# Hybrid state-space and attention layer: branch products per weight block over all tokens, and a later gate for half a branch

## The chip, the cores and the metric

The kernel runs on one core of a Trainium2 chip. The metric is the device time of one launch in microseconds, as the median of several runs. Each engine of the core (PE for matmuls, DVE for vector work, ACT for scalar functions and copies, POOL for the rest, SP for issuing transfers) executes its own instructions in the order in which the program was compiled, and engines wait for each other through semaphores. Matmul results land in PSUM, in banks of 512 float32 columns; all other tiles are in SBUF.

## The reference, cut to what matters

One step of a layer over two streams: 1024 new tokens of one sequence and 64 tokens of a running one, laid side by side as T = 1088 columns.

```python
xn = _rmsnorm(x, p['norm_mix_w'])
z, xbc, dt_raw, q, k, v, gate_ssm, gate_att = split(xn @ p['w_in'])
...
def step(state, inp):
    acum = jnp.cumsum(dtc * a_neg, axis=1)
    seg = acum[:, :, None] - acum[:, None, :]
    decay = jnp.exp(jnp.where(causal, seg, -jnp.inf))
    xdt = xc * dtc[..., None]
    cb = jnp.einsum('blgn,bsgn->blsg', cc, bc)
    y = jnp.einsum('blsg,blsge,bsgep->blgep', cb, decay, xdt)
    y = y + jnp.einsum('blgn,bgepn->blgep', cc, state) * jnp.exp(acum)[..., None]
    to_end = jnp.exp(acum[:, -1:] - acum)
    state = state * jnp.exp(acum[:, -1]) + jnp.einsum('blgn,blge,blgep->bgepn', bc, to_end, xdt)
...
y_ssm = _rmsnorm((y_ssm + d * xs) * silu(z), p['ssm_norm_w'])      # per group of 512
o = _rmsnorm(_diff_attention(q, k_all, v_all, ...), p['subln_w'])  # per head of 128
mix = sigmoid(gate_ssm) * (y_ssm @ p['w_branch_ssm']) + sigmoid(gate_att) * (o @ p['w_branch_attn'])
x = x + mix @ p['w_out']
x = x + conv_ffn(_rmsnorm(x, p['norm_ffn_w']))
```

All inputs and outputs are float32.

## The kernel before, in words

Everything is held feature-major: features on the 128 partitions, tokens along the free axis. Float32 precision is reached by splitting both operands of a product into a rounded part (`hi`) and the rest (`lo`): `product` (L140) issues three matmuls per block of 128 features, hi x hi, hi x lo, lo x hi. A product with 1024 features has 24 matmuls into one PSUM bank. `weights` (L125) loads one 128x1024 weight block (512 KB), casts it on ACT (L136) and subtracts on DVE (L137), into two rotating buffers, with a raised scheduling priority. `acc` (L112) hands out PSUM banks; after the first stage it has two (`pm`).

The stages follow one another roughly so: norm of x, values and time steps, q and k heads, attention (about 560 to 1160 us in the trace), the state-space scan (about 1120 to 1580 us), the branch products, the output product with the second norm (1691 to 1800), the feed-forward part (to the end). The program is a list in priority order; a scheduler with a simulated timeline fixes the order of each engine's instructions when the kernel is built. Work without close dependences is handed out by generators as filler: `fill` (L470) takes a number of steps from the current `filler` after each step of the attention or the scan. In the scan the filler is first what is left of the input projection (`stream`) and, from the tenth of 12 spans on (`BRANCH_AT` = 9), `branch_tiles` (L756); the scheduler may start its work earlier when PE would be idle.

**The scan.** `scan` (L731) goes through 4 groups of 8 heads and 3 spans of 384, 384 and 320 tokens. Each span has 3 calls of `step` (L658), one per 128 tokens (the last has 64), and ends with `gated` (L714). A step loads `bc`, the cumulated decay exponents of 8 heads broadcast over the partitions (L663, 512 KB), and `e2`, their exponentials, two broadcasts to 64 partitions each from the scratch `e_sc` (L664 to L668). PE transposes the inputs (L671, L673) and forms the token products (L674). DVE scales the transposed inputs by the time step into `xdt` and by time step and decay into `xw` (L681). POOL masks `bc` (L682), ACT exponentiates it per head (L684), DVE multiplies (L685), PE forms `yi` (L689), `ye` (L696) and the state update (L702). `e2` multiplies `ye` (L697). `gated` norms the span's output over a group: squares, PE sums (L724), `rstd_of` (L726), four multiplications (L728), a store to `y_sc` (L729).

**The root chain.** `rstd_of` (L209) computes 1/sqrt(mean + eps): ACT Ln (L212) and Exp (L213) for a first value r, then four DVE operations (L214 to L217) for one Newton correction. It is used in the first norm, in the q and k heads (L333), in `gated` and in the second norm (L816).

**The branches.** `branch` (L156) runs three times: attention output `o_sc` with `wba` (branch 1), the first half of the state-space output `y_sc[:D]` with `wbs[0]` (branch 2), both as filler in the scan, and the second half `y_sc[D:]` with `wbs[1]` (branch 3, L784), after the scan. The tokens are cut into two halves of 544. For each half the input is brought into SBUF as 8 blocks of rows, hi and lo (`bring`, L160): branch 1 reads both from `o_sc`; branches 2 and 3 load a staged tile `b_f` (three buffers of 272 columns), cast it on ACT (L169) and subtract on DVE (L170). The tiles `b_hi` and `b_lo` have two buffers, so a later half can come in while an earlier one is multiplied: the second half's rows are issued behind the gate load of weight blocks 2 to 7 (L187 to L190). For each half and each of 8 weight blocks, the gate tile is loaded into `b_g` (L183), for branches 2 and 3 also the running sum (L185), the weight block is loaded and split (L186), and two products of 272 columns follow. DVE reads each result from PSUM as (gate + 1) * product (L196), adds the running sum (L198), and `out` stores it: branch 1 to `m_sc`, branch 2 to `n_sc`, branch 3 through `mixed` (L779), which splits it into hi and lo for the output product. (The stored gate is tanh(g/2); gate + 1 is twice the sigmoid, and the output product is halved at L805.)

Of the kernel before, what the change touches and what calls it, by code (L numbers as in the profile page):

```python
# [42 lines left out]
BG = 4  # L43
LAG = 2
QR = 10
QSQ = 1
BF = 3
# [29 lines left out]
def hybrid_layer(ctx: ExitStack, tc: tile.TileContext, xT, prm, cst, rope, wvd, win, wbs, wba, wout, wup, wdn,  # L77
# [18 lines left out]
    a_sc, e_sc = scratch("a_sc", [32, T]), scratch("e_sc", [32, T])  # L96
# [59 lines left out]
    def branch(stage, pair, src, wts, g0, add, out):  # L156
        def octet():
            return [br.tile([P, 8, HALF], R32, name=n, tag=n, bufs=2) for n in ("b_hi", "b_lo")]

        def bring(c, k, hi, lo):  # L160
            if stage is None:
                for u, t in enumerate((hi, lo)):
                    load(out=t[:, k].bitcast(F32), in_=src[D * u + P * k : D * u + P * (k + 1), c : c + HALF])
                return
            for a in (0, HALF // 2):
                q = slice(a, a + HALF // 2)
                t = stage()
                load(out=t, in_=src[P * k : P * (k + 1), c + a : c + a + HALF // 2])
                S.copy(hi[:, k, q], t)  # L169
                V.tensor_tensor(out=lo[:, k, q], in0=t, in1=hi[:, k, q], op=ALU.subtract)  # L170

        parts = [octet(), None]
        for k in range(8):
            bring(0, k, *parts[0])
        for x, c in enumerate((0, HALF)):
            hi, lo = parts[x]
            if x == 0:
                parts[1] = octet()
            for m in range(KT):
                r = slice(P * m, P * (m + 1))  # L180
                two = pair()
                gt, at = two[:, :HALF], two[:, HALF:T]
                first = load(out=gt, in_=g_sc[g0 + P * m : g0 + P * (m + 1), c : c + HALF])  # L183
                if add is not None:
                    load(out=at, in_=add[r, c : c + HALF])  # L185
                w_hi, w_lo = weights(wts[m], KT, P)  # L186
                if x == 0 and m >= LAG:  # L187
                    with tc.issue_after(first.ins):
                        for k in range(8 * (m - LAG) // (8 - LAG), 8 * (m - LAG + 1) // (8 - LAG)):
                            bring(HALF, k, *parts[1])  # L190
                for a in (0, HALF // 2):
                    q = slice(a, a + HALF // 2)
                    ps = acc(HALF // 2)
                    product(ps, [(w_hi[:, k], w_lo[:, k], hi[:, k, q], lo[:, k, q]) for k in range(KT)])
                    with tc.high_priority(ahead):
                        V.scalar_tensor_tensor(gt[:, q], gt[:, q], 1.0, ps, ALU.add, ALU.mult)  # L196
                if add is not None:
                    V.tensor_tensor(out=gt, in0=gt, in1=at, op=ALU.add)  # L198
                out(m, c, gt)
                yield  # L200

    def store(dst):
        return lambda m, c, t: load(out=dst[P * m : P * (m + 1), c : c + HALF], in_=t)
# [16 lines left out]
    dt_tok, dtw, nacum, decs = (dq.tile([P, 9, 32], F32, name=n) for n in ("dt_tok", "dtw", "nacum", "decs"))  # L220
# [14 lines left out]
    with tc.tile_pool(name="nx", bufs=1) as nx:  # L235
        S.preload_act_table_set(LN_EXP)
        c = 0
        for x, w in enumerate(NORM):
# [6 lines left out]
            if x == 0:  # L245
                load(out=par, in_=prm)
            for k in range(KT):
# [43 lines left out]
    with tc.tile_pool(name="qk", bufs=1) as qk:  # L291
# [66 lines left out]
        def steps():  # L358
# [29 lines left out]
            af, ef = row("af")[:32], row("ef")[:32]  # L388
            for c, w in WIDE:
# [250 lines left out]
    with tc.tile_pool(name="sp", bufs=1) as sp, tc.tile_pool(name="pss", bufs=1, space=PSUM) as pss:  # L640
# [17 lines left out]
        def step(g, ch, o, bx, xs, y, state):  # L658
# [18 lines left out]
            xdt = sp.tile([P, 8, 64], F32, name="xdt", tag="xdt", bufs=2)  # L677
            xw = sp.tile([P, 8, 64], F32, name="xw", tag="xw", bufs=2)
            tr3 = tr[:L].rearrange("p (e q) -> p e q", e=8)
            for dst, sc in ((xdt, dt_tok), (xw, dtw)):  # L680
                V.tensor_tensor(out=dst[:L], in0=tr3, in1=sc[:L, ch, h8].unsqueeze(2).to_broadcast([L, 8, 64]), op=ALU.mult)  # L681
# [71 lines left out]
        def pair():  # L753
            return bs.tile([P, T], F32, name="b_g", tag="b_g", bufs=BG)
# [237 lines left out]
```

## Time and profile before

| what | value |
|---|---|
| median of 3 runs | 2579.67 us (2579.16 to 2581.6) |
| the profiled execution | 2582.58 us, its span 2580.8 us |
| busy: PE, DVE, ACT, POOL | 2525.0, 1399.8, 1032.2, 290.0 us |
| HBM read, written | 263.56 MB, 100.27 MB |
| granted TensorE clock, mean | 0.995 |
| L136, L137 (weight cast, subtract), 220 each | 229.3 us, 284.9 us |
| matmuls on `b_hi` and `b_lo`, 2304 | 228.0 + 227.2 + 227.5 us |

All times of the page are from one profiled execution; the runs' times are without a profile. A matmul's own duration overlaps with the next one's, so counts times start-to-start distance give PE's need, not counts times duration. Idle time of an engine matters only where another one waits for it. The "idle before" column names the instruction that ended the wait.

### The profile page before, as it was taken

To read this page: it belongs to the slowest core of one execution; us is meant where nothing else is said; L and a number is where in the kernel's file an instruction comes from. 1 tells how busy PE (TensorE), PEld (TensorE's weight loads), DVE (VectorE), ACT (ScalarE), POOL (GpSimd) and SP (SyncE) were. 2 spreads that over 40 slices of the span, in tenths; PEclk is the share of its full clock that TensorE was granted. 3 is DMA by queue.
4 is the path that set the end of the run, shared out by engine and by line. 5 is a ranking of instruction groups with operands and counts; after the bars stand their busy time and mean duration, and the time that the engine had idled before them with its cause. 6 is when DMAs were issued, how large, how long until landed. Compare 5 with 4: busy or idle time off the path is not lost.

```text
span 2580.8 us, 41810 instructions
## 1 busy us (share of the span) xinstructions
PE 2525.0 (98%) x16484; PEld 2444.8 (95%) x16484; DVE 1399.8 (54%) x2371; ACT 1032.2 (40%) x2113; POOL 290.0 (11%) x387
## 2 busy tenths in 40 slices
PE   8999999999999999999999989999999999999999
PEld 7999999999999999988788879999999999999999
DVE  7326266654447674665679997658333333343333
ACT  5334234544445554565456643335312222131221
POOL 3000001000001110022333430023000000000000
PEclk9999999999999999999999999999999999999999
DMA  5217167545435433176798978555311111111112
GB/s 162 83 54 282 51 257 213 153 142 148 131 126 164 136 112 111 64 232 192 245 332 258 304 246 272 195 187 193 119 42 47 44 42 50 42 50 40 44 43 77
DMA packets 233685, 366.59 MB, mean 142 GB/s; under 512 B 31184, under 2 KB 160464, under 8 KB 233360
## 3 DMA queue, kind: packets, MB, share of 16 engines
q1 hardware_dynamic: 233488, 363.91, 44.2%
q8 instruction: 130, 2.13, 0.3%
q14 instruction: 67, 0.55, 0.1%
HBM read 263.56 MB, written 100.27 MB: 141 GB/s over the span
## 4 chain that ended last, share of the span: by engine, by line
PE 43%; DMA 3%; DVE 3%; ACT 1%; issue 1%; SPq 0%; POOL 0%; DVEq 0%; ACTq 0%; POOLq 0%
PE mm L143 7%; PE mm L145 7%; PE mm L144 7%; PE up L143 7%; PE up L145 7%; PE up L144 7%; DMA in<-x_sc 1%; DMA b_hi<-o_sc 1%; DVE w_lo L137 1%; PE yi L689 1%; PE stp L702 0%; ACT bc L684 0%; DVE y L728 0%; DMA in<-z_sc 0%; DVE b_lo L170 0%
## 5 line engine op out<-in xcount | busy, mean ns | idle before, releaser
L143 PE MATMUL mm<-xn_hi,w_hi 128*128 128x320 f32 (+1 forms) x1496 | 497.9, 333 | 2.3 <-ACT zr L428 1.1
L145 PE MATMUL mm<-xn_hi,w_lo 128*128 128x320 f32 (+1 forms) x1496 | 496.8, 332 | 0.0
L144 PE MATMUL mm<-xn_lo,w_hi 128*128 128x320 f32 (+1 forms) x1496 | 494.6, 331 | 0.0
L136 ACT CAST w_hi<-w_f 128x1024 fp32r<-128x1024 f32 (+2 forms) x220 | 229.3, 1042 | 547.2 <-PE mm L144 369.3
L137 DVE TENSOR_TENSOR w_lo<-w_f,w_hi 128x1024 fp32r<-128x1024 f32 (+2 forms) x220 | 284.9, 1295 | 300.8 <-ACT w_hi L136 298.4
L143 PE MATMUL up<-x_hi,w_hi 128*128 128x384 f32 (+1 forms) x1056 | 345.0, 327 | 2.7 <-ACT x_hi L820 2.7
L144 PE MATMUL up<-x_lo,w_hi 128*128 128x384 f32 (+1 forms) x1056 | 344.8, 327 | 0.0
L145 PE MATMUL up<-x_hi,w_lo 128*128 128x384 f32 (+1 forms) x1056 | 343.3, 327 | 0.0
L143 PEld LDWEIGHTS mm<-xn_hi,w_hi 128*128 128x128 f32 x1496 | 281.9, 188 | 7.9 <-issue 2.8
L145 PEld LDWEIGHTS mm<-xn_hi,w_lo 128*128 128x128 f32 x1496 | 281.6, 188 | 2.9 <-issue 1.9
L144 PEld LDWEIGHTS mm<-xn_lo,w_hi 128*128 128x128 f32 x1496 | 281.8, 188 | 2.6 <-issue 1.3
L143 PE MATMUL mm<-b_hi,w_hi 128*128 128x272 f32 x768 | 228.0, 298 | 19.1 <-DVE b_g L196 15.9
L144 PE MATMUL mm<-b_lo,w_hi 128*128 128x272 f32 x768 | 227.2, 296 | 0.7 <-DMA b_lo<-o_sc 0.7
L145 PE MATMUL mm<-b_hi,w_lo 128*128 128x272 f32 x768 | 227.5, 297 | 0.0
L143 PEld LDWEIGHTS up<-x_hi,w_hi 128*128 128x128 f32 x1056 | 198.7, 188 | 3.1 <-ACT x_hi L820 3.0
L144 PEld LDWEIGHTS up<-x_lo,w_hi 128*128 128x128 f32 x1056 | 198.8, 188 | 0.1
L145 PEld LDWEIGHTS up<-x_hi,w_lo 128*128 128x128 f32 x1056 | 198.5, 188 | 0.0
L880 DVE TENSOR_TENSOR xa<-xa,mm 128x384 f32<-128x384 f32 x144 | 76.5, 531 | 197.3 <-PE mm L145 197.3
L144 PE MATMUL mm<-f_lo,w_hi 128*128 128x384 f32 (+1 forms) x528 | 173.1, 328 | 0.0
L143 PE MATMUL mm<-f_hi,w_hi 128*128 128x384 f32 (+1 forms) x528 | 173.0, 328 | 0.0
L145 PE MATMUL mm<-f_hi,w_lo 128*128 128x384 f32 (+1 forms) x528 | 173.0, 328 | 0.0
L143 PEld LDWEIGHTS mm<-b_hi,w_hi 128*128 128x128 f32 x768 | 147.3, 192 | 25.4 <-DVE b_g L196 15.4
(252 smaller groups left out, 4803.7 us busy)
## 6 DMA issues: line engine op xcount, KB each, us to landing
w_f<-in_win_dram SPq DMA_DIRECT2D x76, 512.0 KB, 4.0
w_f<-in_wup_dram SPq DMA_DIRECT2D x44, 512.0 KB, 3.7
bc<-a_sc SPq DMA_DIRECT2D x32, 512.0 KB, 6.3
w_f<-in_wbs_dram SPq DMA_DIRECT2D x32, 512.0 KB, 4.2
b_g<-g_sc SPq DMA_DIRECT2D x48, 272.0 KB, 4.5
w_f<-in_wout_dram SPq DMA_DIRECT2D x24, 512.0 KB, 3.8
x_sc<-cc SPq DMA_DIRECT2D x48, 192.0 KB, 1.9
kh_t<-k_st SPq DMA_DIRECT2D x32, 272.0 KB, 6.9
```

The lines of the kernel that those rows point to most:

```text
L136: S.copy(hi, w)
L137: V.tensor_tensor(out=lo, in0=w, in1=hi, op=ALU.subtract)
L143: PE.matmul(ps, a_hi, b_hi, start=i == 0, stop=False)
L144: PE.matmul(ps, a_hi, b_lo, start=False, stop=False)
L145: PE.matmul(ps, a_lo, b_hi, start=False, stop=i == n - 1)
L689: PE.matmul(yi[u : u + 64, e // 2, :L], xdt[:L, e], bc[:L, e, :L], start=True, stop=True)
L880: V.tensor_tensor(out=xa[:, m, c : c + w], in0=xa[:, m, c : c + w], in1=ps, op=ALU.add)
```

## The change: what it does

- `branch` no longer cuts the tokens into two halves. Its input is brought as three pieces of 384, 384 and 320 tokens, all before the first product in program order, each with one buffer per piece (`b_hi0`, `b_lo0` and so on). The loop over weight blocks is outermost, so each block is loaded and split once per branch and serves all three pieces. `TURNS` puts blocks 0 and 1 together, then 2, 3, 4, 5 alone, then 6 and 7 together; in a pair each piece is used for both blocks before the next piece.
- Every product has 384 or 320 columns. `b_f` and `b_g` become tiles of 384 columns; `b_g` has 8 buffers, one tile per load. The generator yields once per product and piece, 24 times a branch instead of 16.
- Branch 2 has no gate and no running sum: ACT copies the product from PSUM, and it is stored to `n_sc`. Branch 3 adds `n_sc` to its product, multiplies by (gate + 1), and adds `m_sc`.
- `rstd_of` computes the correction with one ACT Square and two DVE operations; its result has the opposite sign, and the columns of the norm weights (both norms of x, the state-space norm, the q and k norms) are negated once, by three DVE operations after the parameters' load.
- `e_sc` is gone. `e2` is computed by ACT from `bc`, two exponentials of 64 partitions and 4 x 128 columns, before POOL masks `bc`.
- `dt_tok` and `dtw` lie in one tile, and one DVE operation writes `xdt` and `xw`.

```diff
-BG = 4
-LAG = 2
+BG = 8
+TURNS = ((0, 1), (2,), (3,), (4,), (5,), (6, 7))
...
+    def branch(stage, side, src, wts, gates, adds, out):
+
+        parts = [[br.tile([P, 8, w], R32, name=f"{n}{x}", tag=f"{n}{x}") for n in ("b_hi", "b_lo")]
+                 for x, (c, w) in enumerate(WIDE)]
+        for (c, w), (hi, lo) in zip(WIDE, parts):
+            for k in range(8):
+                if stage is None:
+                    for u, t in enumerate((hi, lo)):
+                        load(out=t[:, k].bitcast(F32), in_=src[D * u + P * k : D * u + P * (k + 1), c : c + w])
+                else:
+                    t = stage()[:, :w]
+                    load(out=t, in_=src[P * k : P * (k + 1), c : c + w])
+                    S.copy(hi[:, k], t)
+                    V.tensor_tensor(out=lo[:, k], in0=t, in1=hi[:, k], op=ALU.subtract)
+        for ms in TURNS:
+            wt = [weights(wts[m], KT, P) for m in ms]
+            for (c, w), (hi, lo) in zip(WIDE, parts):
+                for m, (w_hi, w_lo) in zip(ms, wt):
+                    beside = []
+                    for d, r0 in ([(g_sc, gates)] if gates is not None else []) + [(d, 0) for d in adds]:
+                        t = side()[:, :w]
+                        load(out=t, in_=d[r0 + P * m : r0 + P * (m + 1), c : c + w])
+                        beside.append(t)
+                    to = beside[0] if beside else side()[:, :w]
+                    ps = acc(w)
+                    product(ps, [(w_hi[:, k], w_lo[:, k], hi[:, k], lo[:, k]) for k in range(KT)])
                     with tc.high_priority(ahead):
-                        V.scalar_tensor_tensor(gt[:, q], gt[:, q], 1.0, ps, ALU.add, ALU.mult)
-                if add is not None:
-                    V.tensor_tensor(out=gt, in0=gt, in1=at, op=ALU.add)
-                out(m, c, gt)
-                yield
+                        if not beside:
+                            S.copy(to, ps)
+                        elif not adds:
+                            V.scalar_tensor_tensor(to, to, 1.0, ps, ALU.add, ALU.mult)
+                        else:
+                            V.tensor_tensor(out=beside[1], in0=beside[1], in1=ps, op=ALU.add)
+                    if adds:
+                        V.scalar_tensor_tensor(to, to, 1.0, beside[1], ALU.add, ALU.mult)
+                        V.tensor_tensor(out=to, in0=to, in1=beside[2], op=ALU.add)
+                    out(m, c, to)
+                    yield
...
         act(u, mean, AF.Ln, bias=eps_t[: out.shape[0]], scale=scale)
         act(r, u, AF.Exp, scale=-0.5)
-        V.tensor_scalar(u, mean, -0.5 * scale, -0.5 * EPS, ALU.mult, ALU.add)
-        V.tensor_tensor(out=u, in0=u, in1=r, op=ALU.mult)
-        V.tensor_tensor(out=u, in0=u, in1=r, op=ALU.mult)
-        V.scalar_tensor_tensor(out, u, 1.5, r, ALU.add, ALU.mult)
+        act(u, r, AF.Square, scale=math.sqrt(0.5 * scale))
+        V.scalar_tensor_tensor(u, mean, EPS / scale, u, ALU.add, ALU.mult)
+        V.scalar_tensor_tensor(out, u, -1.5, r, ALU.add, ALU.mult)
...
                 load(out=par, in_=prm)
+                for a, b in ((O_MIX, O_CW), (O_SN, O_D), (O_QN, O_FW)):
+                    V.tensor_scalar_mul(par[:, a:b], par[:, a:b], -1.0)
...
-                act(ef[:, c : c + w], pf[:32, :w], AF.Exp)
             load(out=a_sc, in_=af)
-            load(out=e_sc, in_=ef)
...
-            ev = e_sc.rearrange("(j u) t -> u j t", u=2)
             for u in range(2):
-                src = ev[u, 4 * g : 4 * g + 4, c0 : c0 + L].unsqueeze(0).to_broadcast([64, 4, L])
-                load(out=e2[64 * u : 64 * u + 64, :, :L], in_=src)
+                half = slice(64 * u, 64 * u + 64)
+                act(e2[half, :, :L], bc.rearrange("p (j u) t -> p u j t", u=2)[half, u, :, :L], AF.Exp)
...
-            for dst, sc in ((xdt, dt_tok), (xw, dtw)):
-                V.tensor_tensor(out=dst[:L], in0=tr3, in1=sc[:L, ch, h8].unsqueeze(2).to_broadcast([L, 8, 64]), op=ALU.mult)
+            V.tensor_tensor(out=xx[:L], in0=tr3, in1=dtt[:L, :, ch, h8].unsqueeze(3).to_broadcast([L, 2, 8, 64]), op=ALU.mult)
...
-            yield from branch(None, pair, o_sc, wba, D, None, store(m_sc))
-            yield from branch(stage, pair, y_sc[:D], wbs[0], 0, m_sc, store(n_sc))
+            yield from branch(None, side, o_sc, wba, D, (), store(m_sc))
+            yield from branch(stage, side, y_sc[:D], wbs[0], None, (), store(n_sc))
...
-    run(branch(stage, pair, y_sc[D:], wbs[1], 0, n_sc, mixed))
+    run(branch(stage, side, y_sc[D:], wbs[1], 0, (n_sc, m_sc), mixed))
```

More of the change, by code (lines that the diff above doesn't have):

```diff
@@ L202, in store @@
     def store(dst):
-        return lambda m, c, t: load(out=dst[P * m : P * (m + 1), c : c + HALF], in_=t)
+        return lambda m, c, t: load(out=dst[P * m : P * (m + 1), c : c + t.shape[1]], in_=t)
     def run(gen):
@@ L387, in steps @@
             V.tensor_tensor(out=dtw, in0=dtw, in1=dt_tok, op=ALU.mult)
[L388 removed]
+            af = row("af")[:32]
             for c, w in WIDE:
@@ L750, in stage, with side @@
         def stage():
-            return bs.tile([P, HALF // 2], F32, name="b_f", tag="b_f", bufs=BF)
-        def pair():
-            return bs.tile([P, T], F32, name="b_g", tag="b_g", bufs=BG)
+            return bs.tile([P, 384], F32, name="b_f", tag="b_f", bufs=BF)
+        def side():
+            return bs.tile([P, 384], F32, name="b_g", tag="b_g", bufs=BG)
         def branch_tiles():
```

51 lines of the change are left out of this document (8 added, 43 removed).

## The prediction

> **What bounds the kernel now.** The page comes first: it says that PE is busy 98% of the span, but a busy share cannot say how fast the matmuls follow one another. So the stage table comes next, cut where the first matmul on a `b_hi` piece starts (1265.7), where branch 3 starts (1594.5) and where it ends (1691).
>
> ```profile
> 1265.70:1594.50 328.80, 304.47 (x2373) 273.70 (x2374) 287.15 (x411) 176.61 (x355) 119.33 (x74) 0.97 0.89 287
> 1594.50:1691.00 96.50, 96.50 (x769) 96.50 (x768) 58.67 (x95) 32.49 (x47) 0.00 (x0) 1.00 0.60 195
> ...
> 1800.00:2581.00 781.00, 777.41 (x4704) 777.14 (x4704) 287.76 (x443) 184.99 (x291) 29.07 (x86) 1.00 0.16 53
> ```
>
> The columns are PE, PEld, DVE, ACT, POOL, granted clock, DMA share, GB/s. Branches 1 and 2 and two thirds of the scan share 328.8 us in which DVE is 87% busy, the DMA engines 89%, and the clock drops below 1. Branch 3 and the feed-forward part run with nothing in PE's way. The timeline of PE gives the true price of a matmul, which is start to start:
>
> ```profile
> 1600.16 0.29 PE L143 MATMUL mm<-b_hi,w_hi 128*128 128x272 f32 x1
> 1600.28 0.28 PE L144 MATMUL mm<-b_lo,w_hi 128*128 128x272 f32 x1
> ...
> 1900.15 0.34 PE L143 MATMUL mm<-f_hi,w_hi 128*128 128x384 f32 x1
> 1900.32 0.34 PE L144 MATMUL mm<-f_lo,w_hi 128*128 128x384 f32 x1
> ...
> 1904.75 0.31 PE L143 MATMUL mm<-f_hi,w_hi 128*128 128x320 f32 x1
> 1904.90 0.31 PE L144 MATMUL mm<-f_lo,w_hi 128*128 128x320 f32 x1
> ```
>
> Over longer runs this is 0.1255 us for 272 columns (320 matmuls in the 40 us from 1640), 0.173 for 384 and 0.146 for 320; the lines' 0.29 to 0.34 are latency. What holds PE up between 1265.7 and 1594.5 is read from its waits, and from the clock around the gaps:
>
> ```profile
> PE mm L143 <- DVE b_g L196: 15.9, 8, 4.6
> PE tr L671 <- ACT in L653: 2.8, 4, 1.2
> PE yi L689 <- DVE bc L685: 1.6, 1, 1.6
> ```
>
> (us in total, times, longest), and
>
> ```profile
> 1384.00:1391.00 7.00, 5.85 (x26) 5.85 (x27) 2.73 (x5) 0.73 (x3) 0.00 (x0) 0.51 0.64 196
> ...
> 1304.00:1309.00 5.00, 4.43 (x23) 4.47 (x24) 4.96 (x8) 4.39 (x10) 2.97 (x2) 0.66 1.09 361
> 1532.00:1538.00 6.00, 5.27 (x26) 4.77 (x26) 6.00 (x11) 0.89 (x1) 0.03 (x1) 0.72 0.96 313
> ```
>
> One wait stands out: PE has two accumulation banks, and eight times it finds both unread because DVE is behind with L196. The clock then falls: 7 x 0.49 + 5 x 0.34 + 6 x 0.28 = 6.8 us lost on top of the 15.9. The timeline puts 8.7 us of the waits (2.5, 4.6, 1.6) and the first two dips (5.1 us) into branch 1, and 7.2 us and 1.7 us into branch 2. What DVE does there:
>
> ```profile
> L137 DVE TENSOR_TENSOR w_lo<-w_f,w_hi 128x1024 fp32r<-128x1024 f32 x31 | 51.8, 1672 | 2.9 <-ACT w_hi L136 2.8
> ...
> L170 DVE TENSOR_TENSOR b_lo<-b_f,b_hi 128x272 fp32r<-128x272 f32 x48 | 28.4, 618 | 3.9 <-ACT b_hi L169 3.9
> ...
> L196 DVE SCALAR_TENSOR_TENSOR b_g<-b_g,mm 128x272 f32<-128x272 f32 x63 | 26.6, 426 | 10.0 <-PE mm L145 9.9
> ```
>
> So branch 1, branch 2 and the scan are bound by PE's amount of work plus some 45 us of stalls: 64 products x 24 x 0.1255 = 193 us, 24.5 scan steps x about 3.6 us and nine L724 pairs of 0.5 us make 92 us (a step from the timeline: tr 0.44, cb 0.33, yi 1.0, ye 0.8, stp 0.86, some 0.2 for the changes between them), so 285 of 328.8.
>
> **The change, part by part.** *Piece widths.* Per weight block 4 x 24 x 0.1255 = 12.05 us become 48 x 0.173 + 24 x 0.146 = 11.81. Over 24 blocks that is **-5.9 us** of PE, about 2 per branch. *Weight blocks used once.* 48 loads with their L136 and L137 become 24. In the stage that takes away 16 x 1.67 = 27 us of DVE, 16 x 1.04 = 17 us of ACT, 8.4 MB. *Branch 2 ungated.* L196 (32 x 0.43) and L198 (16, 13 us) leave DVE, 27 us; ACT takes 24 reads of PSUM at about 0.45 (L428, 128x320: 0.428). Gate and m_sc loads, 32 x 0.28 = 9 MB, leave the stage; branch 3 adds m_sc. *Root chain.* Nine times L214 to L217 (0.53 + 0.62 + 0.63 + 0.76) become two DVE operations of about 0.7 and one ACT of 0.5: -10 us of DVE, +4.5 of ACT. *One scaling for xdt and xw.* 25 x (0.68 + 0.675) becomes one operation of 1024, taken at 1.22 by L543's 128x1024 read of PSUM: -3.4 us. *Branch 3's prefetch* (16 L170, 10 us) leaves the stage, since single buffers forbid it. DVE goes from 287 to about 287 - 27 - 27 - 10 - 3 - 10 = 210 us, 66% of a stage of 318. *Decay from rows.* 25 x 2 loads of e_sc (6 MB) go; ACT gets 50 exponentials of 64 x 512, each between 0.38 (L684, 128 elements) and 1.42 (L720, mostly 1536); taken 0.58 from L700, whose 512 elements are the nearest: +29 us (+71 at the upper end, ACT then at 76%, still beside PE's work). ACT ends near 177 - 17 + 11 + 4.5 + 29 - 6 = 199 us, 62%: hidden. DMA falls by 8.4 + 9 + 6 + 2 of 94 MB.
>
> On the path each step waits longer: bc's landing (6.8 us), then the two exponentials (1.2 us), then POOL's L682, since L682 overwrites bc. ACT is in order, so weight casts and branch 2's evacuations queue behind an exponential whose bc is late. L684 waits 34.8 us for L682 already, with three bc buffers ahead of it and branch matmuls to cover it: **0**, bounds -3 (DVE's wait of 1.1 for e_sc and some landing time go) and +10.
>
> *What DVE's relief gives.* Branch 2's banks are read by ACT: 7.2 + 1.7 us go. In branch 1 DVE still reads them, with a quarter less to do: half of 13.8. **-16 us**, bounds 0 and -22.7. A page of the Trainium skill weighs the dips otherwise: TensorE: Matmul & The Clock Gate, Part 1, halves the clock after an idle window of about 3.4 us. By that alone only the 4.6 us gap would cost its dip, 3.4 of the 6.8 us, and the gain would be 7.2 and half of 12.1, 13 us for 16 (sum -7.4); the trace has dips behind gaps of 2.5 and 2.2 us, and decides.
>
> *Pieces held once.* The three pieces of a branch have one buffer each, so the next branch can fill a piece only after blocks 6 and 7 have used it. Bringing 24 blocks of rows through three b_f buffers costs c / 3 each, with c a buffer's round from issue over landing and L169 to the end of L170. In the quiet of branch 3 c is 5.2 us (third load of a set at 1605.9, its subtract over at 1611.1), in the scan about 10 (1462.8 to 1473.4). Covered are about 50 us (15.3 of products after piece 0 is free, 7 of scan; then two pieces of 8.3 with 8 of scan beside; the first products of piece 2 the rest). Branch 2 stalls by 8c - 50: nothing at 5.2, 30 at 10. DVE and DMA a quarter lighter put c near 7.2: **+8 us**. Branch 3 meets no scan: piece 0 is free 15.3 us ahead, piece 2 is asked for 16.6 us after branch 2's end, 32 us in all, and 24 x 5.2 / 3 = 42 less the last piece's own work and the three loads in flight gives **+3** (bounds 0 and +10). Branch 1 needs 3.1 MB before its first product instead of 4.4, but all 8.7 MB in its first 24 us of products instead of half: **0**, bounds -5 and +8.
>
> *Weight handover.* After the pair (0, 1), and into the next branch, a new block's cast and subtract (1.04 + 1.22 quiet, 1.67 busy) must fit into one 320-wide product of 3.5 us, where 6 us were free before. Waits on L136 are 1.5 us now: **+2**, bounds 0 and +6. *Elsewhere* the last L212 chain before the feed-forward part and the first norm lose one DVE operation each (0.5 and 0.4), both head blocks about as much: **-1.5**. The negated parameter columns wait for par (lands 9.0 us in) in a DVE gap from 8.3 to 10.8: **0**, up to +2 if they are put ahead of the squares. Branch 3's DVE work rises to 24 x (0.55 + 0.6 + 0.55 + 0.55) + 13 + 10 = 77 of 97 us, PSUM reads first: **0**, up to +5.
>
> Sum: -5.9 - 16 + 8 + 3 + 2 - 1.5 = **-10.4**. The profiled execution took 2582.58 us (span 2580.8, 1.8 around it), 2.9 above the median of the runs, 2579.67; the same difference on the median gives **2569.3**.
>
> **Rivals.** *A: everything opens up* (chance 0.23). With DVE at two thirds all waits for L196 and their dips go (-22.7), half of the stage's other PE idle time of about 12 us goes (-6), and rounds of 5 to 6 us stall nothing: with -5.9 and -1.5 that is -36, **2543.5**. For it: branch 3 and the feed-forward part show PE without gaps where DVE is 61% and 37% busy. Against it: from 1160 to 1260 DVE is at 48%, and PE still loses some 10 us in small waits behind scan steps.
>
> *B: slower, at the start of branch 2* (0.22). With c at 10, as in the scan now, the stall is 30 instead of 8: +22, **2591**. It decides from c = 8.5, where 8c - 50 eats the -10.4. For it: DMA landings in the scan have a median of 5.6 us for 136 KB, and the new loads are 192 KB; the subtract that frees a buffer stands behind scan work in DVE's order. Against it: today's rounds belong to prefetches that nobody waits for.
>
> *C: nothing to measure* (0.15): the scan itself, through POOL and ACT (L684 behind L682 34.8 us, now behind two more exponentials), paces branch 2, and DVE's freed time is idle; about half the -16 goes, with +3 of extra stall: **2580**.
>
> **How the numbers follow.** The forecast has 0.40, its own range 2562 to 2577. A measurement tells apart about 0.2%, 5 us. Faster: 0.35 of the forecast and A, 0.58. Within: 0.04 and C's 0.14, 0.18. Slower: B and the ends, 0.24. The range runs from A's centre to B's, 2544 to 2591, and leaves a tenth beyond each.
>
> **What would show it.** PE's wait for the first product's bank in the stage falls from 15.9 us to under 8; branch 3's products start near 1584 instead of 1594.5 and take about 97 us; DVE's share of the stage is near 66%; c is 6 to 8 us. PE waiting for `b_hi` or `b_lo` by over 20 us makes the prediction wrong on B's side, exponentials waiting for bc with PE idle on C's.

## The result, and the profile after

The changed kernel takes 2603.18 us (median of 4 runs, 2601.23 to 2605.43), the kernel before 2580.64 us on the same chips: a ratio of 1.0086 with a 95% interval of 1.0074 to 1.0098. It is slower by 22 us where 10 us less were forecast, and it lies outside the range. One launch each of the kernel before, of e4 and of e5 was far slower (8752, 3065 and 3509 us) and is left out of the numbers below. The profiled executions differ by 20.4 us of span (2601.2 against 2580.8), so the profile can be asked where they went.

A table of the times at which PE reaches the same instruction in both traces answers most of it:

| PE reaches | before | after | later by |
|---|---|---|---|
| the first projection matmul | 20.0 | 26.8 | 6.8 |
| the first `mm<-xn_hi,w_hi` (the q and k heads, behind values and time steps) | 83.3 | 89.1 | 5.8 |
| the 81st score matmul of the attention | 495.3 | 505.9 | 10.6 |
| the scan's first `yi` | 1131.9 | 1145.8 | 13.9 |
| the first product on `b_hi` | 1265.7 | 1272.4 | 6.7 |
| the scan's last `yi` | 1545.9 | 1537.6 | -8.3 |
| the output product | 1691.1 | 1713.7 | 22.6 |
| the end | 2580.8 | 2601.2 | 20.4 |

(The attention begins earlier than the 560 us given above: its first score matmul before the change is at 410.0.) Two stretches lose time: everything up to the scan (13.9 us) and the branch stage itself (441.3 us for 425.4, +15.9). Half of the first loss comes back before the branches begin: from the scan's first `yi` to the first product on `b_hi` PE takes 126.6 us for 133.8. Of the experiments below, e5 and e8, which compute the decay factors from `bc`, take 126.9 and 127.1 us there, e3 and e6, which load them again, 132.5 and 131.8; so this gain goes with the decay rows. The feed-forward part gives 2 us back.

First the stage table of the changed kernel, cut at the first product on `b_hi`, at the start of branch 3 and at its end. The columns are PE, PEld, DVE, ACT, POOL, granted clock, DMA share, GB/s:

```profile
1272.40:1616.60 344.20, 306.64 (x1994) 271.24 (x1994) 224.79 (x287) 210.20 (x412) 113.20 (x74) 0.95 0.64 204
1616.60:1713.70 97.10, 96.02 (x577) 94.86 (x578) 64.10 (x113) 25.67 (x45) 0.00 (x0) 1.00 0.66 205
```

DVE fell from 87% to 65% of the first window, as forecast (66%), and the DMA share from 0.89 to 0.64. Yet PE stands for 37.6 us of it instead of 24.3, and the mean clock is lower (a part of its half-clock time falls into PE's own waiting). Two busy resources were relieved, and the engine that sets the end waits longer. Branch 3 needs 97.1 us, as forecast. The waits of PE in the same stretch (us in total, times, longest) say for whom it stands:

```profile
PE mm L143 <- DVE b_g L186: 15.2, 2, 13.3
PE tr L665 <- ACT in L648: 8.0, 5, 3.6
PE ye L689 <- DVE state L702: 4.6, 3, 2.4
PE cb L667 <- ACT in L648: 3.5, 1, 3.5
```

The wait for DVE's read of PSUM (L186, before L196) is still 15 us, but eight waits have become essentially one, of 13.3 us. It ends at 1316.7. SP's part of the timeline shows what was late (start, duration, instruction; L164 loads a block of rows, L177 a gate tile):

```profile
1304.05 0.58 SPq L164 DMA_DIRECT2D b_hi<-o_sc  x1
1304.67 0.53 SPq L164 DMA_DIRECT2D b_lo<-o_sc  x1
1305.24 0.69 SPq L177 DMA_DIRECT2D b_g<-g_sc  x1
```

All 48 loads of the three pieces stand in SP's queue ahead of the first gate tile: from 1269.95 to 1305.2, 35 us. PE begins the first product at 1272.4, has filled its two banks by 1291.7, does the scan steps that are ready, and stands from 1303.4: no result can be read without a gate. And when the gate has landed (6.2 us after its issue, at 1311.5), DVE is in the span's closing work for another 4.6 us:

```profile
1307.80 8.36 DVE L721 SCALAR_TENSOR_TENSOR y<-y,par,grs 128x384 f32<-128x384 f32 x4
1316.09 0.54 DVE L186 SCALAR_TENSOR_TENSOR b_g<-b_g,mm 128x384 f32<-128x384 f32 x1
...
1307.38 3.67 POOL L712 TENSOR_TENSOR y<-y,in 128x1536 f32<-128x1536 f32 x1 [2.32 <-DVE y L711]
1311.00 1.41 POOL L675 TENSOR_SCALAR_AFFINE_SELECT bc<-bc 128x1024 f32<-128x1024 f32 x1
1312.64 1.84 POOL L714 TENSOR_TENSOR in<-in 128x768 f32<-128x768 f32 x1 [0.23 <-ACT in L713]
1314.56 1.19 POOL L715 TENSOR_TENSOR in<-in 128x384 f32<-128x384 f32 x1
```

Four multiplications that fill 2.20 us when nothing of POOL runs beside them (at 1331.05) fill 8.36 us beside POOL's operations. Each of the four ends 0.41 or 0.42 us after one of the four POOL operations above; the first takes 3.66 us, beside the 3.67 us of L712. The Trainium skill (SBUF — State Buffer, "Who interferes with whom") says that a VectorE instruction with two SBUF inputs contends with a GpSimd instruction that reads SBUF, and calls the ports that they share an exclusive lock; these rows agree, and here it is VectorE that waits.

The other loss is at the very start. SP's queue before, and after:

```profile
11.73 1.38 SPq L242 DMA_DIRECT2D xc<-in_xT_dram  x3
13.15 0.43 SPq L135 DMA_DIRECT2D w_f<-in_wvd_dram  x1
```

```profile
11.62 8.38 SPq L237 DMA_DIRECT2D xc<-in_xT_dram  x11
20.04 2.01 SPq L135 DMA_DIRECT2D w_f<-in_wvd_dram  x4
```

Before, the first weight block's load went out just ahead of a group of eight input loads that must wait for a free buffer; after, it stands just behind that group, which waits until 16.35 and issues until 20.0. The projection starts 6.8 us later.

### The profile page after: what moved, and what is told of

The parts are those of the page before. It is cut to its first block, busy times and chain, and to the rows that moved or that the text cites. A ratio compares the mean times of both kernels' runs of the same rounds, so it can differ in the third digit from the quotient of the medians.

```text
span 2601.2 us, 40477 instructions
## 1 busy us (share of the span) xinstructions
PE 2528.9 (97%) x15908; PEld 2443.4 (94%) x15908; DVE 1324.2 (51%) x2222; ACT 1078.2 (41%) x2206; POOL 283.7 (11%) x387
## 4 chain that ended last, share of the span: by engine, by line
PE 44%; DMA 4%; ACT 3%; issue 2%; DVE 2%; POOL 1%; SPq 0%; ACTq 0%; DVEq 0%; POOLq 0%
PE mm L143 7%; PE mm L145 7%; PE mm L144 7%; PE up L143 7%; PE up L145 7%; PE up L144 7%; DMA in<-x_sc 2%; DMA bc<-a_sc 1%; ACT bc L677 1%; ACT in L648 1%; DMA b_f<-y_sc 1%; PE stp L695 1%; DVE b_lo L169 0%; ACT e L662 0%; PE yi L682 0%
## 5 line engine op out<-in xcount | busy, mean ns | idle before, releaser
L137 DVE TENSOR_TENSOR w_lo<-w_f,w_hi 128x1024 fp32r<-128x1024 f32 (+2 forms) x196 | 248.1, 1266 | 318.9 <-ACT w_hi L136 316.1
L136 ACT CAST w_hi<-w_f 128x1024 fp32r<-128x1024 f32 (+2 forms) x196 | 204.2, 1042 | 466.5 <-PE mm L144 304.7
L143 PE MATMUL mm<-b_hi,w_hi 128*128 128x384 f32 (+1 forms) x576 | 193.8, 337 | 17.4 <-DVE b_g L186 15.2
L144 PE MATMUL mm<-b_lo,w_hi 128*128 128x384 f32 (+1 forms) x576 | 193.6, 336 | 0.5 <-DVE b_lo L169 0.4
L145 PE MATMUL mm<-b_hi,w_lo 128*128 128x384 f32 (+1 forms) x576 | 192.0, 333 | 1.1 <-DVE w_lo L137 0.9
L452 DVE SCALAR_TENSOR_TENSOR cc<-pre,par,cc 128x384 f32<-128x384 f32 (+1 forms) x216 | 128.3, 595 | 44.1 <-ACT cc L450 41.0
```

The source lines that it names most:

```text
L136: S.copy(hi, w)
L137: V.tensor_tensor(out=lo, in0=w, in1=hi, op=ALU.subtract)
L143: PE.matmul(ps, a_hi, b_hi, start=i == 0, stop=False)
L144: PE.matmul(ps, a_hi, b_lo, start=False, stop=False)
L145: PE.matmul(ps, a_lo, b_hi, start=False, stop=i == n - 1)
L452: V.scalar_tensor_tensor(cc[:, :m], pre[:, i : i + m], cw(i), cc[:, :m], ALU.mult, ALU.add)
```

## The experiments

All ratios are to the kernel before, run on the same chip. Single executions of one kernel spread by some 4 us to either side (e5: 2574.8 to 2582.8), so a span from one profile settles nothing under about 5 us; waits and places in a queue are read from it, sizes from the ratios.

**e1, gates first.** The gate tiles of the first two weight blocks are loaded ahead of the piece that they belong to:

```diff
+        early = {}
...
         for x, ((c, w), (hi, lo)) in enumerate(zip(WIDE, parts)):
+            if x == 0 or not adds:
+                for m in TURNS[0]:
+                    early[m, c] = sides(m, c, w)
...
+                    beside = early.pop((m, c), None)
+                    if beside is None:
+                        beside = sides(m, c, w)
```

> The changed kernel with one edit: the gate tiles of the first two weight blocks are loaded ahead of the piece that they go with, instead of behind all 48 loads of the pieces. Theory G (the first two products of branch 1 cannot leave PSUM because their gate is issued at 1305 us, behind 48 piece loads on SP's in-order queue): the 13.3 us wait of PE goes, and with it the two half-clock stretches around it (3.4 and 13.7 us long, 8.5 us lost); median 2582 to 2589. Rival D (the transfers of the pieces bound the start of branch 1, whatever stands in front of them): PE waits for b_hi or b_lo instead, median 2597 or more.

2588.89 us (10 runs), ratio 1.0031 (1.0021 to 1.0040), span 2589.1. The output product is 9.9 us later than before instead of 22.6. Its waits from 1263 to 1620 us:

```profile
PE tr L676 <- ACT in L659: 13.7, 4, 4.8
PE mm L143 <- DMA b_hi<-o_sc: 4.6, 3, 2.8
PE mm L143 <- DVE b_g L197: 2.4, 2, 1.5
```

The wait for the gate fell from 15.2 to 2.4 us, and about 14 us of the time with it (1.0086 to 1.0031). A part came back at once as waits for Silu'd inputs (`tr` and `cb` together), 14.7 us for 11.5.

**e2, the old root chain.** The four DVE operations return, without the negated parameters:

```diff
-        act(u, r, AF.Square, scale=math.sqrt(0.5 * scale))
-        V.scalar_tensor_tensor(u, mean, EPS / scale, u, ALU.add, ALU.mult)
-        V.scalar_tensor_tensor(out, u, -1.5, r, ALU.add, ALU.mult)
+        V.tensor_scalar(u, mean, -0.5 * scale, -0.5 * EPS, ALU.mult, ALU.add)
...
-                    V.tensor_scalar_mul(par[:, a:b], par[:, a:b], -1.0)
```

> The changed kernel with the root chain of before (four vector operations, no negated parameters). Theory S (the edit of the root chain moves the first weight load one place later in SP's order, behind the group of input loads that waits for a buffer, and the first projection starts at 26.8 us instead of 20.0): the first projection starts near 20 us again and the median falls by 4 to 8, to 2595 to 2599. Rival N (the start is late for another reason, or the time comes back later): first projection near 26 us, or median 2601 to 2605.

2594.33 us, ratio 1.0051 (1.0036 to 1.0066), span 2591.0: some 9 us less. The projection starts at 20.5, the scan 1.9 us later than before instead of 13.9. The gate wait stays (14.0 us).

**e3, the branch part alone, and e4, all but it.** e3 is the kernel before with the new `branch`; e4 the changed kernel with the old one.

> The kernel before with the branch change alone (pieces, weight blocks used once, branch 2 ungated), with the old root chain, decay transfers and two scalings. Theory G+S: first projection at 20 us, the 13 us wait for the first gate there, the time from the start of branch 1 to the output product longer than before by 8 to 16 us; median 2586 to 2597. Rival (the loss in the scan comes from the exponentials of the decay rows on ACT): the stage is as fast as before or faster, median 2568 to 2581.

> The changed kernel with the branches of before (halves, prefetch, all gated): root chain, decay rows and merged scaling alone. Theory G+S: the start loses its 6 us and about 5 more at the start of the attention, the scan gains some from fewer transfers and vector operations; median 2580 to 2592. Rival (the exponentials on ACT slow the scan): the stage from branch 1's first product to the output product is over 5 us longer than before, median above 2595.

e3 takes 2598.0 us, ratio 1.0068 (1.0045 to 1.0092), just above the 2586 to 2597 expected: the first product comes as early as before, the output product 13.5 us later. Its order of work differs, and the loss sits at the same place under another name:

```profile
PE gst L717 <- POOL in L715: 15.7, 2, 10.5
PE mm L143 <- DVE b_g L186: 5.3, 2, 4.3
```

Here PE's next instruction is the span's sum, not a product, so the same stretch is booked to POOL; both banks are full from 1286.4, the first gate lands at 1317.0, and no third product could begin before. The clock is at half for 20.5 us from 1299. e4 takes 2582.31 us (9 runs), ratio 1.0001 (0.9990 to 1.0011); it starts 6.2 us late and is 12.5 us late at the scan, and wins back 9 us behind that.

**e5, both repairs** (e1 and e2 together).

> The changed kernel with both repairs: gate tiles ahead of the pieces, and the root chain of before. Theory G+S: the two losses are in different places and add up (12 to 14 us and 9 us): first projection at 20 us, first product of branch 1 near 1260, median 2578 to 2583, so what is left of the change is worth nothing. Rival (the losses overlap, since the scan stage takes up what was late before it): median 2585 or more.

2578.96 us (11 runs), ratio 0.9992 (0.9981 to 1.0003), span 2576.6. The two losses add up, and what is left of the change is worth nothing that can be told from zero. Stage table and waits:

```profile
1263.30:1591.40 328.10, 302.69 (x1995) 266.28 (x1995) 231.39 (x305) 198.66 (x400) 117.40 (x74) 0.98 0.66 214
```

```profile
PE tr L675 <- ACT in L658: 5.6, 4, 3.6
PE ye L699 <- DVE state L712: 3.4, 2, 2.9
PE mm L143 <- DMA b_hi<-o_sc: 2.8, 2, 2.5
PE mm L143 <- ACT b_hi L181: 2.7, 1, 2.7
PE mm L145 <- DVE w_lo L137: 2.6, 2, 2.1
PE mm L143 <- DVE b_g L197: 2.0, 2, 1.5
PE stp L705 <- DVE xx L684: 2.0, 1, 2.0
```

This is the most telling view of the case. PE's waits for DVE's reads of PSUM are down from 15.9 to 2.0 us, DVE is at 71% instead of 87%, and PE still stands for 25.4 us of 328.1, 24.3 of 328.8 before. Several smaller waits have taken the place of one. No run takes the parts of the new `branch` (wider pieces, weight blocks used once, branch 2 without a gate) apart, so what each is worth alone is not shown.

**e6 to e8, the decay rows and the exponentials on ACT.** e6 is e5 with `e2` loaded from `e_sc` again. e7 is e5 with the next span's Silu one step earlier. e8 is the kernel before with the decay rows and the merged scaling alone.

```diff
-                act(e2[half, :, :L], bc.rearrange("p (j u) t -> p u j t", u=2)[half, u, :, :L], AF.Exp)
+                load(out=e2[64 * u : 64 * u + 64, :, :L], in_=src)
...
-GATE_AT = 2
+GATE_AT = 1
```

> The kernel with both repairs, and the decay factors as transfers from their scratch again instead of two exponentials a step. Theory A (the exponentials make ACT's Silu of the next span late, and PE waits for it at the first transposes of a span, with half clock after): PE's waits of the transposes for Silu fall from some 16 us in the stage to under 6, and the stage from branch 1's first product to the output product is 5 us or more shorter than with both repairs alone; the steps before branch 1 lose about 5 us again; median 2572 to 2581. Rival (the Silu is late because the scan as a whole runs faster, the exponentials have no part in it): those waits stay above 10 us and the median is 2582 or more.

> The kernel with both repairs, and the Silu of the next span placed behind the second step of a span instead of the third. Theory A2 (what is left in the stage is PE waiting for a Silu that comes one step too late): the waits of the transposes for it fall under 4 us and the median falls to 2566 to 2576. Rival (ACT has no room: the Silu and its two table loads then delay the exponentials of the third step): PE waits for bc or for b_cb instead, median 2580 or more.

> The kernel before with the decay factors from the broadcast rows and the one scaling operation alone (old branches, old root chain). From the run without the branch change: it lost about 11 us ahead of the scan to the root chain and ended 3 later, so without the root chain it should be 5 to 9 us faster than before: median 2571 to 2577. Rival (there is nothing in these two edits, the 8 us came from the root chain's own shorter work in the scan): 2578 to 2583.

e6: 2583.89 us, ratio 1.0012 (1.0003 to 1.0020). The waits for Silu'd inputs are 11.0 us in its stage, 6.6 in e5, so taking the exponentials off ACT does not remove them; the waits for branch 1's pieces rise from 2.8 to 7.1 us with the extra transfers. The decay rows are worth some 5 us in this company. e7: 1.0020 (1.0011 to 1.0028), not better; the waits for Silu are 7.0 us in the stage, under 4 expected, and a wait of 4.9 us for ACT's `zr` appears at 1210.7. e8: 0.9993 (0.9983 to 1.0004); the gain that I expected of these two parts alone was not there, and 14 us of waits for L196 were. Its waits for Silu'd inputs are 9.9 us, for 3.0 before, so the exponentials or the merged scaling do seem to raise them in that company; what causes them stays open. e4 is e8 with the new root chain, and the two differ by 2 us: with the old branches most of what the chain loses ahead of the scan comes back in it.

**e9 to e12, one Silu, and the first weight's place.** ACT's timeline in e5 ahead of its longest wait, PE at 1462.1, shows exponentials between the two halves of one Silu, at the price of two more table loads:

```profile
1452.78 1.28 ACT L658 ACT_TABLE_LOAD   x1 [2.76 <-DMA in<-x_sc]
1454.08 1.81 ACT L658 ACTIVATE in<-in 128x1920 f32<-128x1920 f32 x1
1455.90 1.28 ACT L672 ACT_TABLE_LOAD   x1
1457.20 1.27 ACT L672 ACTIVATE e<-bc 64x512 f32<-64x512 f32 x2
...
1458.99 1.28 ACT L658 ACT_TABLE_LOAD   x1
1460.28 1.80 ACT L658 ACTIVATE in<-in 128x1920 f32<-128x1920 f32 x1
```

The changed kernel has three such places. e9 is the changed kernel with one Silu for a span, e11 e5 with it. e10 is e1 with its new root chain kept and a higher priority for all weight loads of the first stages, e12 is e10 with one Silu.

```diff
-SPLIT = 5
+SPLIT = 10
...
-AHEAD_IN = 100
+AHEAD_IN = 130
```

> The changed kernel, with Silu of a span's inputs as one ACT operation of 10 x 384 instead of two of 5 x 384. In the scan of the changed kernel ACT loads its function table 32 times, 24 before the change: three times exponentials of a scan step stand between the two halves of one Silu (at 1314, 1376 and 1466 us), each costing two more table loads of 1.28 us; the two longest waits of PE for Silu'd inputs (3.55 us at 1379.5, 3.56 us at 1475.9) end beside two of them, each with a clock dip of 3.4 us. Theory A, the swaps hold up PE: 24 loads in the scan, these two waits and dips go, about 2 x (3.55 + 1.7) = 10.5 us, a span near 2591 and a ratio near 1.0045. Theory B, the waits come from late loads of the inputs or from ACT's load: the waits stay near 15 us in all, the span stays within 3 us of 2601 and the ratio near 1.0086. The gate wait of 13.3 us stays under both.

> The changed kernel with the gate tiles of the first two blocks loaded ahead of their piece (as in e1) and its new root chain kept, but the weights' priority raised by 130 in place of 100, which puts the first weight block's load back to the place in SP's list that it had before the change (the eighth). Theory A, the new chain costs at the start only through that place: the first projection starts near 20.5 us instead of 26.3, the half-clock stretch at 28.6 goes, and the span comes 5 to 7 us below the 2589.1 of e1, 2582 to 2584, a ratio near 1.001; what is lost at the start of the attention (PE waiting 3.5 us for p_t near 429) stays. Theory B, the chain's own operations are late: the first projection stays above 25 us, and the span near 2589.

> The kernel of e5 (both repairs), with Silu of a span as one operation. One pair of table loads too many is left there (1456 to 1462 us), with PE's longest wait of the stage behind it, 3.57 us, and a clock dip. Theory A: it goes, the span falls from 2576.6 by about 5 to 2571 to 2573, and the ratio to before from 0.9992 to about 0.997. Theory B: the wait is only moved, or one Silu of twice the length holds up ACT's other readers as much, the ratio stays within 0.9985 to 1.0005.

> The kernel of e10 (gates first, new root chain, first weight block back in its place) with Silu as one operation. If the three losses add up (place of the first weight, gates, table loads), it comes 3 to 8 us below e10, near 2577, a ratio of 0.998 to 1.000, and near e11 but for the attention's start, some 3 to 5 us. If the table loads cost nothing, it equals e10 within 2 us.

e9: 2607.36 us, 1.0104 (1.0090 to 1.0119); e11: 1.0038 (1.0025 to 1.0052); e12: 1.0052 (1.0039 to 1.0064). The one Silu is a miss, by the ratios 5 us worse on the changed kernel (the intervals overlap) and 12 us on the repaired ones. The table loads fell to 24 in the scan, but the one operation takes 3.4 us and waits for more loads: in e11, PE waits for it 3.9 us at 1121, 3.0 at 1186 and 4.2 at 1454, and ahead of the first and the third ACT had waited for the load of z (5.5 and 8.1 us).

e10: 2583.28 us, 1.0008 (0.9999 to 1.0017), span 2579.6. The first weight block is back in its place:

```profile
11.66 1.85 SPq L248 DMA_DIRECT2D xc<-in_xT_dram  x4
13.56 0.90 SPq L135 DMA_DIRECT2D w_f<-in_wvd_dram  x2
```

The projection starts at 21.1 with the new chain in the kernel. So at the start the chain's operations cost next to nothing; the place of one load did. At the attention's start 5.9 us are still lost (0.9 us late ahead of it, 6.8 at the 81st score matmul), with PE waiting 3.8 us for `p_t`, 2.0 before. With the old chain the same stretch loses nothing in e2 and 1 us in e5. The traces say where the time goes: between the first and the 81st score matmul PE stands 4.2 us longer in e10 than before, and the half clock costs 1.7 us more. They also show another order of work: some 18 matmuls of the projection that ran ahead of the first score matmul now run behind it, in e10 as in the changed kernel, e1, e4 and e14, and not in e2 and e5. Why the shorter chain leads to that order stays open.

**e13 to e16, Silu cut after the sixth block.** The first operation then covers all of x, which the transposes read, and the second only z, which the span's end needs: e5, e10, the kernel before and the changed kernel with

```diff
-                for u in range(0, 10, SPLIT):
-                    last = act(t[:, u : u + SPLIT, :w], t[:, u : u + SPLIT, :w], AF.Silu)
+                for u, v in ((0, 6), (6, 10)):
+                    last = act(t[:, u:v, :w], t[:, u:v, :w], AF.Silu)
```

> The kernel of e5 (both repairs), with the two Silu operations of a span cut after 6 of the 10 blocks instead of after 5: the first then covers all that the transposes read (blocks 0 to 5, from x), the second only z, which the span's end needs. In e5 PE waits 7.8 + 1.0 us for Silu'd inputs, the longest time (3.57 us at 1462.1) because exponentials stand between the two operations. Theory A, these waits are the second operation's lateness: they fall below 4 us, the dips behind them go, span near 2571 (-5), ratio near 0.997. Theory B, the inputs themselves come too late, or another wait takes the place: span within 3 us of 2576.6, ratio 0.998 to 1.001.

> The kernel of e10 with Silu cut after the sixth block. In e10 PE waits some 15 us for Silu'd inputs (3.18 at 1436.4, 3.11 at 1468.6, 4.38 at 1505.4 the longest) with half-clock stretches of 6.8, 3.4 and 6.8 us beside them (8.5 us lost). Theory A: half or more of it goes, span near 2569 (-11), ratio near 0.997. Theory B: 2579.6 within 3 us, ratio 1.000 to 1.002.

> The kernel before with Silu cut after the sixth block, as a control. PE waits there 4.3 us for Silu'd inputs in all and 15.9 us for DVE's reads of PSUM. If the input is no bound before the change, the ratio is within 0.999 to 1.001 (a gain of 2 to 3 us at most). If it falls by 0.3% or more, the cut is a general gain and says nothing of the change.

> The changed kernel with Silu cut after the sixth block and nothing else. Its waits for Silu'd inputs are 11.2 + 3.5 us, its gate wait 13.3 us and the late start of 6.8 us stay. Theory A: 8 to 13 us less than 2601.2 with the dips behind the waits, span 2588 to 2593, ratio near 1.004. Theory B: 2601 within 3 us, ratio near 1.0086.

e13: 2581.09 us, 0.9993 (0.9982 to 1.0003). e14: 1.0007 (0.9997 to 1.0016). e15, the control: 1.0019 (1.0009 to 1.0029), so the cut is no gain of its own and costs 5 us there. e16: 2599.03, 1.0066 (1.0051 to 1.0082), by the ratios about 5 us less than the changed kernel (the intervals overlap), under the 8 to 13 expected. In e14 the waits for Silu'd inputs fell from 13 us in e10 to 2.4, and the time stayed (waits from 1263 to 1620 us):

```profile
PE mm L145 <- DVE w_lo L137: 3.6, 2, 3.3
PE mm L143 <- ACT b_hi L181: 3.3, 2, 2.3
PE yi L693 <- DVE bc L689: 3.0, 2, 2.3
PE cb L678 <- ACT b_cb L681: 2.5, 2, 2.0
PE tr L676 <- ACT in L659: 2.4, 3, 1.5
PE stp L706 <- ACT b_cb L681: 2.0, 2, 1.2
```

A second kind of wait was taken away. Others of the scan step's own chain (transpose, copy, multiplication, product, state) and of the weights came in its place, but not for all of it: PE's idle time in the stage fell from 25.9 us in e10 to 19.6 in e14. What ate the rest is the clock, at half for 23.9 us of the stage instead of 17.1. No version beats the kernel before by what can be measured; e4, e5, e8, e10, e13 and e14 equal it.

## Why the prediction was wrong, step by step

**The bound was read rightly.** PE's amount of work plus stalls set the stage, and no transfer or other engine paced it. The share of the stalls was read too large: the "some 45 us" are what the counted work left over, while the trace before has 24.3 us of idle PE and 17.1 us at half clock (8.5 us lost, one stretch at 1489.9 not counted), so some 11 us were work that the prices missed and that no repair of a wait could win.

**The step that failed most: branch 1's first products.** "Branch 1 needs 3.1 MB before its first product instead of 4.4, but all 8.7 MB in its first 24 us of products instead of half: 0, bounds -5 and +8." The step counted bytes and not places in SP's queue. With all three pieces brought ahead of the loop, 48 loads, 0.73 us from one to the next with other loads between, stand ahead of the first gate tile, 35 us in all. Measured, for a forecast of 0: a wait of 13.3 us, with the clock at half for 5.6 us of work behind it (2.8 us lost), and about 14 us less in e1 once the gates go first. Both halves of this were in the diff: the loop that brings the pieces now lies wholly ahead of the loop that loads `b_g`.

**The step that failed next: the root chain "elsewhere".** Forecast -1.5, with up to +2 for the negated columns. The DVE operations saved were counted, and not that a shorter chain gives the scheduler another order. e2 measures the chain with its negations at +9 us in the changed kernel; e10 shows that at the start it is one load's place. The second half, at the attention's start, is measured but not explained. With the old branches (e4 against e8) the whole chain costs 2 us, so a lateness ahead of the scan is not yet a loss at the end.

**The term of the sum that was not there: -16 from DVE's relief.** The relief itself came as forecast (65%, and PE's waits for its and ACT's reads of results are 2.0 and 1.1 us in e5), the gain did not: PE's idle time in the stage is 25.4 us in e5 for 24.3. The view of waits names for each stop the one that ended last; I took the sum of that line for what can be won. That others were due close behind it is what e5 and e14 suggest; no run shows how close. The time at half clock in the stage went from 17.1 to 13.7 us, which is 1.7 us won of the 6.8. Rival C's result, no measurable change, was wrong for the change as it stood; its 2580 is where the repaired kernel is, but for a cause that the trace does not show (exponentials waiting for `bc` with PE idle), so that is luck.

**Right in size.** Piece widths: in branch 3 the distances are 0.173 and 0.146 us as taken from the feed-forward part,

```profile
1654.10 0.31 PE L144 MATMUL mm<-b_lo,w_hi 128*128 128x320 f32 x1
1654.24 0.31 PE L145 MATMUL mm<-b_hi,w_lo 128*128 128x320 f32 x1
...
1657.02 0.33 PE L143 MATMUL mm<-b_hi,w_hi 128*128 128x384 f32 x1
1657.19 0.33 PE L144 MATMUL mm<-b_lo,w_hi 128*128 128x384 f32 x1
```

and its 24 products need 94.5 us of PE by these distances (an estimate), 2 less than before, so the price is right (its factors give -5.8 for three branches, not -5.9). As time it shows less: branch 3 takes 97.1 us for 96.5, with 2.2 us of waits in it, and PE's busy time in the stage is only 1.8 us lower in e5, where two branches should give 3.8; the transposes and the state update of one scan step, some 1.3 us, stand in the stage after the change and ahead of it before. The waits for new weights (`w_lo`) are nothing in the stage and 0.9 us in branch 3, in e5 2.6 and 0.9, for +2. The merged scaling takes 1.215 us (taken 1.22), the exponentials 0.628 (0.58), ACT's copy of a result 0.48 (0.45). The exponentials at 0 hold: removing them does not help (e6).

**Branch 2's staging, +8, and rival B.** B was right about the round, and wrong about the stall: a buffer's round was 10.4 us in the median of branch 2's 24 blocks, for which 8c - 50 gives 33 us, and PE waited 0.4 us for `b_lo` (2.7 for `b_hi` in e5). The cover was mis-sized. I had worked it out at 50 us; in the trace the staging begins at 1464.6, 32 us ahead of branch 2's first product (1496.7), and the first product on the third piece starts at 1535.3, since the last scan steps run between the four products before it: 71 us of cover. There was nothing to spare: the last of the 24 blocks was ready at 1537.0, 1.7 us into that product. So the side was B's, and its mechanism played no part. That the forecast's +8 was not paid is luck of the order, since the cover was not the one worked out. The branch 3 staging, +3, shows as no wait for `b_hi` or `b_lo` after the change and as 0.5 us in e5.

## What to carry to other kernels

When loads are gathered ahead of a loop, count every small load that now stands behind them in the same queue, in issue time, and ask who reads it first; bytes saved say nothing of that. A line in a table of waits, with the half clock behind it, is at best an upper bound of what its removal gives (e1 won 14 us of a wait of 13.3 and a dip of 2.8). Where several engines hand work round in short steps the removal can give nothing: take the wait away and see which is next. A saving of a few instructions can change the compiled order far from it, so compare the places of the first loads before trusting a term of -1.5 us.

## What the runs showed of the hardware that was not expected

PE's clock falls behind gaps much shorter than the stretch at half clock that follows. In e13 two products begin after waits of 1.63 and 1.60 us,

```profile
1308.56 0.42 PE L143 MATMUL mm<-b_hi,w_hi 128*128 128x320 f32 x1 [1.63 <-DVE b_g L197]
...
1594.45 0.44 PE L143 MATMUL mm<-b_hi,w_hi 128*128 128x384 f32 x1 [1.60 <-ACT b_g L195]
```

and the clock is at half for 3.4 us from 0.5 and 1.4 us after each start (third number from the right):

```profile
1309.10:1312.50 3.40, 3.40 (x15) 3.40 (x14) 3.36 (x3) 1.09 (x2) 3.20 (x2) 0.50 1.05 330
1595.80:1599.20 3.40, 3.40 (x13) 3.40 (x12) 2.25 (x3) 1.79 (x3) 0.00 (x0) 0.51 0.88 248
```

The Trainium skill (TensorE: Matmul & The Clock Gate, Part 1) puts the fall behind an idle window of about 3.4 us; the length of the stretch agrees, the gap needed does not. Whether a given short gap costs its 1.7 us varied: the wait of 2.9 us at 1403 in the changed kernel was followed by such a stretch, the wait of 2.9 us at 1477 in e5 was not.

The traces show most of what decides. In each of the 18, the half-clock stretches start at moments that lie a whole number of 3.413 us apart, to within 0.002 us, so each execution can be cut into windows of that length. Taking those from 40 to 2560 us that begin at full clock: where PE was idle for more than 1.9 us of the window, the next one was at half clock in 93 cases of 93; with 1.2 to 1.9 us idle, in 27 of 149; with less, in 3 of 12,839. The gap at 1403 lies within one such window of the changed kernel, in which PE is busy for 1.07 us, and the next is at half clock (first number behind the comma PE's busy time, third from the right the clock):

```profile
1400.81:1404.22 3.41, 1.07 (x4) 0.49 (x4) 1.90 (x2) 1.34 (x4) 2.29 (x3) 1.00 0.09 26
1404.22:1407.64 3.42, 3.42 (x10) 2.08 (x9) 1.63 (x3) 3.36 (x10) 1.35 (x2) 0.50 0.72 210
```

The gap at 1477 in e5 is split between two windows, with PE busy for 2.08 and 1.79 us, and costs nothing:

```profile
1472.46:1475.88 3.42, 2.08 (x23) 1.58 (x21) 3.42 (x1) 0.96 (x3) 3.31 (x1) 1.00 0.00 0
1475.88:1479.29 3.41, 1.79 (x10) 1.39 (x11) 3.41 (x6) 2.08 (x4) 1.83 (x2) 1.00 0.18 50
```

So a gap of 2 to 3 us has no fixed price in these traces; it depends on how the gap falls into the windows, and where the first window begins after the program's start differs from trace to trace.
